# A bidirectional hybrid block on one core: transposes of FFN blocks grouped and moved behind the next gate job's first quantum, those of mLSTM outputs and merged branches grouped

## Chip, core and metric

One Trainium2 chip, one of its cores. The metric is the device time of one execution in microseconds (us). The engines are named as the profile names them: PE (TensorE, matmuls) with PEld (its weight loads), DVE (VectorE), ACT (ScalarE), POOL (GpSimd) and SP (SyncE, which issues most DMAs).

## What is computed

One layer over 256 tokens of width 2048, in float32. A mixer has two branches, a bidirectional mLSTM with 4 heads of width 512 and a bidirectional gated delta rule with 16 heads; their outputs are projected, gated, added and projected again. A SwiGLU feed-forward network (FFN) of inner width 5632 follows, then a final norm. Cut to what matters here:

```python
h_a = rms_norm(h_a, mlstm_norm_w)                       # 4 heads x 512
y_a = (sigmoid(a_o) * h_a) @ w_branch_a
x = x + gate_m * ((g_a * y_a + g_b * y_b) @ w_out)      # merged branches
hf = rms_norm(x, norm_ffn_w) * (1 + scale_f) + shift_f
gt, up = split(hf @ w_gate_up, 2)
x = x + gate_f * ((silu(gt) * up) @ w_down)
return rms_norm(x, norm_final_w)
```

## The kernel before

**Two forms of every number.** A product of two float32 matrices is made of three fast matmuls: each operand is split into a high part (rounded to the fast format) and a low part (the rest), and high x high, low x high and high x low are added. ACT makes the high part with a copy, DVE the low part with a subtraction. So weights arrive as `raw`, become `wh` and `wl` (L213, L215), and activations exist as pairs: `hah`/`hal` (mLSTM output), `mgh`/`mgl` (merged branches), `hfh`/`hfl` (FFN input), `ffh`/`ffl` (FFN inner activations). `split` (L290) makes such a pair from a tile in PSUM.

**Jobs and quanta.** `tjob` (L198) is one projection: all 256 tokens, as two halves of 128, by 512 output columns. For the gate and up projections it goes through 4 chunks of weights, each in two halves. One half is a *quantum*: one `wh`, one `wl` (three buffers each), and 12 matmuls with 512 columns (L247 high x high, L248 low activations x high weights, L249 high x low weights). After each quantum the generator calls `pump` and yields. `pump` (L159) hands out a side job: while the FFN runs, every 8 quanta one product on DVE of a row of `ada` with `crow` (L125), from which the gate row of the last residual is made.

**Transposes.** The result of a job has tokens on the partitions; the next projection needs features there. TensorE transposes each 128 x 128 block into a bank of PSUM (`gps`, L76, four banks, 512 float32 columns each), and ACT and DVE split it from there. Three places do so, each with 8 transposes for 512 features (4 feature blocks `f`, 2 token halves `t`):

- `mlstm` (L982), for each of 4 heads: tile `pxa`, transposes at L1061, then for each feature block a scaled copy on ACT to `hah` (L1065) and a multiply-subtract on DVE to `hal` (L1066). The four steps are written one block after another: two transposes, the copy, the subtraction, then the next block's two transposes, two blocks to a bank. The heads run in pairs (0 with 1, 2 with 3), interleaved piece by piece, beside the jobs `yb`.
- `merged` (L1174), for each of 4 column groups: tile `pxm`, transposes at L1181, called three times during the jobs `ya` (L1257) and once in the first job `o` (L1272). Four transposes to a bank, then a `split` of the bank (L291, L292).
- the FFN loop (L1522), for each of 11 blocks `j`: gate job, up job, then the product `sg` = silu(gate) x up on DVE (L1526, one for each token half), then tile `pxf`, transposes at L1532, four to a bank, and a `split` of each bank to `ffh` and `ffl`. Only the down projection (jobs `d`) reads these.

**What sets the order.** Each engine runs its own stream of instructions in order; engines wait for each other with semaphores. The order within a stream is made when the kernel is built, by a scheduler that plays the program through with its own model of times: of the instructions of an engine that it counts as ready, it takes the one written first. So an instruction that isn't ready there lets later ones pass. `order(ins)` (L72) pins an instruction behind the one written last before it on the same engine; `order(ins, False)` does nothing. Instructions on the same bank of PSUM are kept apart: one that writes into a bank is held until the reads written before it are done, even if they read other columns.

The lines as they stand in the FFN loop:

```python
run(gate(j) if j else gt0)
sg = sgs.pop(j)
run(tjob(f"up{j}", ..., lambda ps: [V.tensor_tensor(sg[:, t], sg[:, t], ps[t], ALU.mult) for t in range(2)]))
for e2 in range(2):
    px = gps(f"pxf{j}_{e2}")
    ...
```

Of the kernel before, what the change touches and what calls it, by code (L numbers as in the profile page):

```python
# [9 lines left out]
F32 = mybir.dt.float32  # L10
F32R = mybir.dt.float32r
AF = mybir.ActivationFunctionType
ALU = mybir.AluOpType
PSUM = bass.MemoryType.PSUM

P = 128
T = 256
# [15 lines left out]
PK_MNW = 128  # L33
# [19 lines left out]
def hybrid_block(ctx: ExitStack, tc: tile.TileContext, xr, nfr, crow, pk_d, cst_d, ada2, ada4, win0, winb, wint, wba, wbb, wo, wgu, wd, out, dbg=None):  # L53
    nc = tc.nc
    V, S, G, PE = nc.vector, nc.scalar, nc.gpsimd, nc.tensor

    def pool(stack, name, bufs=1, **kw):
        return stack.enter_context(tc.tile_pool(name=name, bufs=bufs, **kw))
# [10 lines left out]
    def big(p, dt, name):  # L69
        return p.tile([P, KB, T], dt, tag="b16", name=name)  # L70

    def order(ins, yes=True):  # L72

        return tc.keep_in_program_order(ins) if yes else ins

    def gps(name):  # L76
        return g_ps.tile([P, 512], F32, tag="g", name=name)
# [3 lines left out]
    pk = cp.tile([P, PK_N], F32, name="pk")  # L81
# [8 lines left out]
    ident = cst[:, CS_ID : CS_ID + P]  # L90
# [185 lines left out]
    def run(job):  # L276
        for _ in job:
            pass
# [11 lines left out]
    def split(hi, lo, v):  # L290
        S.activation(hi, v, AF.Copy)  # L291
        V.tensor_tensor(lo, v, hi.bitcast(F32), ALU.subtract)  # L292
# [214 lines left out]
    with ExitStack() as s0:  # L507
# [54 lines left out]
        for b2 in range(KB // 2):  # L562
            px = gps(f"pxx{b2}")
# [418 lines left out]
    def mlstm(h):  # L982
# [52 lines left out]
        hs = ml.tile([P, 2, DV_A], F32, tag="hs", bufs=2, name=f"hs{h}")  # L1035
# [17 lines left out]
        for t in range(2):  # L1053
            V.scalar_tensor_tensor(hs[:, t], hs[:, t], ss[:, t : t + 1], so[:, t], ALU.mult, ALU.mult)
        yield
        for e2 in range(2):
            px = gps(f"pxa{h}_{e2}")
            for e in range(2):
                f = 2 * e2 + e
                for t in range(2):  # L1060
                    PE.transpose(px[:, e * T + t * P : e * T + (t + 1) * P], hs[:, t, f * P : (f + 1) * P], ident)  # L1061
                b = 4 * h + f
                c = pk[:, PK_MNW + b : PK_MNW + b + 1]
                pe_ = px[:, e * T : (e + 1) * T]
                S.activation(hah[:, b], pe_, AF.Copy, scale=c)  # L1065
                V.scalar_tensor_tensor(hal[:, b], pe_, c, hah[:, b].bitcast(F32), ALU.mult, ALU.subtract)  # L1066
        yield

    heads1 = {h: gdn_phase1(h) for h in range(NH_B)}
# [25 lines left out]
    for g in range(4):  # L1095
# [6 lines left out]
        if g == 3:  # L1102
            settle()
            sf.close()
            mq["pool"] = pool(sq_, "mq", side="right")
            first2 = [mlstm(h) for h in range(2)]
            for c in first2:
                next(c)
            o4s = [o_load(0, mq["pool"])]
# [63 lines left out]

    def merged(g, mgh, mgl):  # L1174

        for e2 in range(2):
            px = gps(f"pxm{g}_{e2}")
            for e in range(2):
                f = 2 * e2 + e
                for t in range(2):  # L1180
                    PE.transpose(  # L1181
                        px[:, e * T + t * P : e * T + (t + 1) * P], mg[:, t, g * 512 + f * P : g * 512 + (f + 1) * P], ident
                    )
            b = 4 * g + 2 * e2
            split(mgh[:, b : b + 2], mgl[:, b : b + 2], px.rearrange("p (e t) -> p e t", e=2))

    def y_bs():
        for g in range(4):
# [23 lines left out]
    hah, hal = big(bigD, F32R, "hah"), big(bigD, F32R, "hal")  # L1212
    mg = mgp.tile([P, 2, D], F32, name="mg")
# [6 lines left out]
    drive(cores, 3)  # L1220
    every[0] = 1
    drive(steps(mlstm(2), mlstm(3)), 3)
    fill(1000)
    mgh, mgl = big(bigC, F32R, "mgh"), big(bigC, F32R, "mgl")
# [29 lines left out]
    for g in range(4):  # L1254
        for i, _ in enumerate(y_a(g)):
            if g and i == 3:
                merged(g - 1, mgh, mgl)  # L1257
            if i in (1, 5) and g < 2:
                row_diag(2, 2 * g + i // 4, sr)
            if i in (3, 7) and g < 2:  # L1260
                row_spread(2, 2 * g + i // 4, gm)
# [8 lines left out]
    for _ in range(2):  # L1270
        next(o_first)
    merged(3, mgh, mgl)  # L1272
    sw = ExitStack()
    sd.close()
# [45 lines left out]
    def gate_done(j):  # L1320
        def done(ps):
            sgs[j] = later["pool"].tile([P, 2, 512], F32, tag="sg", bufs=2, name=f"sg{j}")
            for t in range(2):
                S.activation(sgs[j][:, t], ps[t], AF.Silu)
        return done

    def gate(j):
        return tjob(f"gt{j}", [wgu[j, 0, u] for u in range(4)], Late("h"), Late("l"), gate_done(j), 0 if j else 2, steps=2, lead=None if j else xq)
# [9 lines left out]
    gt0 = gate(0)  # L1338
# [179 lines left out]
    ffh = fp.tile([P, FB, T], F32R, name="ffh")  # L1518
    ffl = fp.tile([P, FB, T], F32R, name="ffl")
    every[0] = 8  # L1520

    for j in range(FB // 4):  # L1522
        run(gate(j) if j else gt0)
        sg = sgs.pop(j)
        run(tjob(f"up{j}", [wgu[j, 1, u] for u in range(4)], hfh, hfl,
                 lambda ps: [V.tensor_tensor(sg[:, t], sg[:, t], ps[t], ALU.mult) for t in range(2)]))  # L1526
        for e2 in range(2):
            px = gps(f"pxf{j}_{e2}")
            for e in range(2):
                f = 2 * e2 + e  # L1530
                for t in range(2):
                    PE.transpose(px[:, e * T + t * P : e * T + (t + 1) * P], sg[:, t, f * P : (f + 1) * P], ident)  # L1532
            b = 4 * j + 2 * e2
            split(ffh[:, b : b + 2], ffl[:, b : b + 2], px.rearrange("p (e t) -> p e t", e=2))

    sh.close()
    dp = pool(ctx, "dp", side="right")
    gf = dp.tile([P, D], F32, name="gf")
# [30 lines left out]
    for g in range(4):  # L1569
        c = slice(g * 512, (g + 1) * 512)  # L1570
# [119 lines left out]
```

## Time and profile before

| | us |
|---|---|
| median of 3 runs | 1951.5 (1947.19 to 1954.09) |
| the profiled execution, its own time | 1949.33 |
| its span in the trace | 1947.5 |
| DVE busy | 1406.7 |
| ACT busy | 1033.8 |

The mean granted clock of TensorE in the profiled execution is 0.997 of full speed. The span reaches from the first to the last instruction of the trace. A line of the timeline reads: start in us, duration in us, engine, line of the kernel, operation, output tile <- input tiles, shapes, how many such in a row (xN), and in brackets how long the engine was idle before it and what it waited for. The durations of matmuls overlap, because they are pipelined; what one costs is read from start to start. A line of the waits reads: engine, tile and line, what it waited for, then the total in us, how many times, and the longest. The tile names are without the number of the block or head, so `pxf` is all of `pxf0_0` to `pxf10_1`.

### The profile page before, as it was taken

Reading aid. Unit: us, or ns where it says so; the run is one execution under the profiler, and the core shown is the slowest. Engines: PE = TensorE matmul, PEld = TensorE weight load, DVE = VectorE, ACT = ScalarE, POOL = GpSimd, SP = SyncE. Lnnn points to the kernel's source line nnn. Section 1 sums busy time; section 2 is a strip of 40 time slices with the busy share of each in tenths; the row PEclk is TensorE's granted clock in tenths of the full one; section 3 lists DMA queues with packets and bytes.
Section 4 is the critical chain, followed back from the end, with each engine's and each line's share of the span. In section 5 each row is a group of like instructions: output and inputs, shape, how many; then the busy total and the mean of one; then the engine's idle time right before and its main releaser. Section 6 shows DMA issues by size and latency. Waiting matters only on the chain.

```text
span 1947.5 us, 27217 instructions
## 1 busy us (share of the span) xinstructions
PE 1919.7 (99%) x10436; PEld 1699.3 (87%) x10436; DVE 1406.7 (72%) x2084; ACT 1033.8 (53%) x1564; POOL 124.1 (6%) x223
## 2 busy tenths in 40 slices
PE   8999999999999999999999999999999999999997
PEld 6888889998999899889788888888888888888886
DVE  6788886898788789876577988766666565555554
ACT  3147656775776587565544444644444444444443
POOL 0001220111011101120100000200000000000000
PEclk9999999999999999999999999999999999999999
DMA  9997676667676766686777998576667665655563
GB/s 399 420 358 236 188 256 249 214 224 238 219 220 204 241 220 238 208 293 245 268 289 266 351 353 314 195 263 245 246 239 260 239 219 199 204 207 209 196 208 137
DMA packets 80774, 485.68 MB, mean 249 GB/s; under 512 B 11434, under 2 KB 17138, under 8 KB 26626
## 3 DMA queue, kind: packets, MB, share of 16 engines
q1 hardware_dynamic: 64368, 451.02, 63.9%
q0 software_dynamic: 8672, 17.88, 4.3%
q10 hardware_dynamic: 7602, 15.03, 2.0%
q8 instruction: 82, 1.34, 0.3%
q14 instruction: 50, 0.40, 0.1%
HBM read 467.07 MB, written 16.82 MB: 248 GB/s over the span
## 4 chain that ended last, share of the span: by engine, by line
PE 90%; DMA 4%; DVE 3%; ACT 2%; issue 1%; SPq 0%; DVEq 0%; ACTq 0%
PE acc_up L247 4%; PE acc_up L249 4%; PE acc_up L248 4%; PE acc_gt L248 4%; PE acc_d L248 4%; PE acc_gt L249 4%; PE acc_d L247 4%; PE acc_d L249 4%; PE acc_gt L247 4%; DMA ra<-ada 3%; PE acc_b L186 3%; PE acc_o L247 3%; PE acc_o L248 3%; PE acc_o L249 3%; PE acc_b L188 3%; PE acc_b L187 3%
## 5 line engine op out<-in xcount | busy, mean ns | idle before, releaser
L215 DVE TENSOR_TENSOR wl_d<-raw_d,wh_d 128x1024 fp32r<-128x1024 f32 x88 | 107.7, 1225 | 105.9 <-ACT wh_d L213 105.9
L215 DVE TENSOR_TENSOR wl_up<-raw_up,wh_up 128x1024 fp32r<-128x1024 f32 x88 | 107.7, 1225 | 100.7 <-ACT wh_up L213 100.7
L215 DVE TENSOR_TENSOR wl_gt<-raw_gt,wh_gt 128x1024 fp32r<-128x1024 f32 x88 | 107.7, 1224 | 78.6 <-ACT wh_gt L213 78.6
L186 PE MATMUL acc_b<-hh,wh_b 128*128 128x256 f32 x576 | 161.9, 281 | 0.0
L213 ACT ACTIVATE wh_d<-raw_d 128x1024 fp32r<-128x1024 f32 x88 | 92.9, 1056 | 126.5 <-PE acc_d L248 117.7
L188 PE MATMUL acc_b<-hh,wl_b 128*128 128x256 f32 x576 | 158.7, 276 | 0.0
L187 PE MATMUL acc_b<-hl,wh_b 128*128 128x256 f32 x576 | 158.3, 275 | 0.0
L213 ACT ACTIVATE wh_gt<-raw_gt 128x1024 fp32r<-128x1024 f32 x88 | 92.8, 1055 | 117.1 <-PE acc_gt L248 71.1
L213 ACT ACTIVATE wh_up<-raw_up 128x1024 fp32r<-128x1024 f32 x88 | 92.7, 1055 | 108.1 <-PE acc_up L248 77.1
L125 DVE SCALAR_TENSOR_TENSOR ada<-ada,crow 128x2048 f32<-128x2048 f32 x64 | 146.2, 2284 | 0.0
L247 PE MATMUL acc_up<-wh_up,hfh 128*128 128x512 f32 x352 | 133.4, 379 | 0.0
L248 PE MATMUL acc_up<-wh_up,hfl 128*128 128x512 f32 x352 | 133.4, 379 | 0.0
L249 PE MATMUL acc_up<-wl_up,hfh 128*128 128x512 f32 x352 | 133.4, 379 | 0.0
L247 PE MATMUL acc_gt<-wh_gt,hfh 128*128 128x512 f32 x344 | 131.6, 383 | 0.0
L248 PE MATMUL acc_gt<-wh_gt,hfl 128*128 128x512 f32 x344 | 131.3, 382 | 0.2 <-DVE hfl L1475 0.2
L247 PE MATMUL acc_d<-wh_d,ffh 128*128 128x512 f32 x344 | 130.5, 379 | 0.0
L248 PE MATMUL acc_d<-wh_d,ffl 128*128 128x512 f32 x344 | 130.5, 379 | 0.0
L249 PE MATMUL acc_gt<-wl_gt,hfh 128*128 128x512 f32 x344 | 130.4, 379 | 0.0
L249 PE MATMUL acc_d<-wl_d,ffh 128*128 128x512 f32 x344 | 130.4, 379 | 0.0
L595 PE MATMUL first<-x,raw 128*128 128x256 f32 x488 | 110.1, 386 | 6.0 <-ACT x L587 6.0
L595 PEld LDWEIGHTS first<-x,raw 128*128 128x128 f32 x488 | 92.9, 192 | 23.3 <-ACT x L587 10.7
L187 PEld LDWEIGHTS acc_b<-hl,wh_b 128*128 128x128 f32 x576 | 110.6, 192 | 0.1
(403 smaller groups left out, 5294.7 us busy)
## 6 DMA issues: line engine op xcount, KB each, us to landing
ada<-ada SPq DMA_DIRECT2D x64, 1024.0 KB, 5.2
raw_gt<-wgu SPq DMA_DIRECT2D x44, 1024.0 KB, 5.0
raw_up<-wgu SPq DMA_DIRECT2D x44, 1024.0 KB, 5.0
raw_d<-wd SPq DMA_DIRECT2D x44, 1024.0 KB, 4.9
raw_b<-winb SPq DMA_DIRECT2D x36, 1024.0 KB, 5.6
ra<-ada SPq DMA_DIRECT2D x30, 1025.0 KB, 14.9
raw_z<-wint SPq DMA_DIRECT2D x16, 1024.0 KB, 5.0
raw_v<-wint SPq DMA_DIRECT2D x16, 1024.0 KB, 5.4
```

The lines of the kernel that those rows point to most:

```text
L125: order(V.scalar_tensor_tensor(raw, raw, 1.0, row_c[:, :D], ALU.mult, ALU.mult, accum_out=mod[:, c : c + 1]))
L186: PE.matmul(o, wh[:, k], woven(hh[:, kk]), start=kk == 0, stop=False)
L187: PE.matmul(o, wh[:, k], woven(hl[:, kk]), start=False, stop=False)
L188: PE.matmul(o, wl[:, k], woven(hh[:, kk]), start=False, stop=kk == KB - 1)
L213: order(S.activation(wh, raws[u][:, k0 : k0 + 2], AF.Copy), early)
L215: order(V.tensor_tensor(wl, raws[u][:, k0 : k0 + 2], wh.bitcast(F32), ALU.subtract), early or beside[0])
L247: order(PE.matmul(ps[t], xh[:, kk, c], woven(wh[:, k]), start=kk == 0, stop=False), early and steps > 1)
L248: PE.matmul(ps[t], xl[:, kk, c], woven(wh[:, k]), start=False, stop=False)
L249: PE.matmul(ps[t], xh[:, kk, c], woven(wl[:, k]), start=False, stop=kk == last)
L595: PE.matmul(first[o], raw[:, o], x[:, b], start=b == 0 and o % 2 == 0, stop=b == KB - 1 and o % 2 == 1)
```

## The change

In `mlstm` and `merged` the two banks are taken first, all 8 transposes are written in one go, and the reads follow. Within a group every transpose but the first is pinned with `order` behind the one before it (`f or t` is false only for the first). In the FFN loop the transposes and their `split` become a function `turn`, put aside in `turning`; it is called in the next round of the loop after the gate job's first quantum, that is at its first yield. The turn of the last block is called right after the loop.

```diff
@@ mlstm
-        for e2 in range(2):
-            px = gps(f"pxa{h}_{e2}")
-            for e in range(2):
-                f = 2 * e2 + e
-                for t in range(2):
-                    PE.transpose(px[:, e * T + t * P : e * T + (t + 1) * P], hs[:, t, f * P : (f + 1) * P], ident)
-                b = 4 * h + f
-                c = pk[:, PK_MNW + b : PK_MNW + b + 1]
-                pe_ = px[:, e * T : (e + 1) * T]
-                S.activation(hah[:, b], pe_, AF.Copy, scale=c)
-                V.scalar_tensor_tensor(hal[:, b], pe_, c, hah[:, b].bitcast(F32), ALU.mult, ALU.subtract)
+        px = [gps(f"pxa{h}_{i}") for i in range(2)]
+        for f in range(4):
+            for t in range(2):
+                c = (f % 2) * T + t * P
+                order(PE.transpose(px[f // 2][:, c : c + P], hs[:, t, f * P : (f + 1) * P], ident), f or t)
+        for f in range(4):
+            b = 4 * h + f
+            c = pk[:, PK_MNW + b : PK_MNW + b + 1]
+            pe_ = px[f // 2][:, (f % 2) * T : (f % 2 + 1) * T]
+            S.activation(hah[:, b], pe_, AF.Copy, scale=c)
+            V.scalar_tensor_tensor(hal[:, b], pe_, c, hah[:, b].bitcast(F32), ALU.mult, ALU.subtract)
@@ merged
-        for e2 in range(2):
-            px = gps(f"pxm{g}_{e2}")
...
-            b = 4 * g + 2 * e2
-            split(mgh[:, b : b + 2], mgl[:, b : b + 2], px.rearrange("p (e t) -> p e t", e=2))
+        px = [gps(f"pxm{g}_{i}") for i in range(2)]
+        for f in range(4):
+            for t in range(2):
+                c = (f % 2) * T + t * P
+                order(PE.transpose(px[f // 2][:, c : c + P], mg[:, t, g * 512 + f * P : g * 512 + (f + 1) * P], ident), f or t)
+        for i in range(2):
+            b = 4 * g + 2 * i
+            split(mgh[:, b : b + 2], mgl[:, b : b + 2], px[i].rearrange("p (e t) -> p e t", e=2))
@@ FFN loop
+    turning = []
 
     for j in range(FB // 4):
-        run(gate(j) if j else gt0)
+        for i, _ in enumerate(gate(j) if j else gt0):
+            if turning and not i:
+                turning.pop()()
         sg = sgs.pop(j)
         run(tjob(f"up{j}", [wgu[j, 1, u] for u in range(4)], hfh, hfl,
                  lambda ps: [V.tensor_tensor(sg[:, t], sg[:, t], ps[t], ALU.mult) for t in range(2)]))
-        for e2 in range(2):
-            px = gps(f"pxf{j}_{e2}")
...
-            split(ffh[:, b : b + 2], ffl[:, b : b + 2], px.rearrange("p (e t) -> p e t", e=2))
+
+        def turn(j=j, sg=sg):
+            px = [gps(f"pxf{j}_{i}") for i in range(2)]
+            for f in range(4):
+                for t in range(2):
+                    c = (f % 2) * T + t * P
+                    order(PE.transpose(px[f // 2][:, c : c + P], sg[:, t, f * P : (f + 1) * P], ident), f or t)
+            for i in range(2):
+                b = 4 * j + 2 * i
+                split(ffh[:, b : b + 2], ffl[:, b : b + 2], px[i].rearrange("p (e t) -> p e t", e=2))
+
+        turning.append(turn)
+
+    turning.pop()()
```

More of the change, by code (lines that the diff above doesn't have):

```diff
@@ L1174, in merged @@
     def merged(g, mgh, mgl):
-        for e2 in range(2):
-            px = gps(f"pxm{g}_{e2}")
[L1178 to L1183, printed above, removed]
-            b = 4 * g + 2 * e2
-            split(mgh[:, b : b + 2], mgl[:, b : b + 2], px.rearrange("p (e t) -> p e t", e=2))
+        px = [gps(f"pxm{g}_{i}") for i in range(2)]
[6 more added lines that the diff above has]
+            split(mgh[:, b : b + 2], mgl[:, b : b + 2], px[i].rearrange("p (e t) -> p e t", e=2))
     def y_bs():
@@ L1526, in hybrid_block @@
                  lambda ps: [V.tensor_tensor(sg[:, t], sg[:, t], ps[t], ALU.mult) for t in range(2)]))
-        for e2 in range(2):
-            px = gps(f"pxf{j}_{e2}")
-            for e in range(2):
-                f = 2 * e2 + e
+        def turn(j=j, sg=sg):
+            px = [gps(f"pxf{j}_{i}") for i in range(2)]
+            for f in range(4):
                 for t in range(2):
-                    PE.transpose(px[:, e * T + t * P : e * T + (t + 1) * P], sg[:, t, f * P : (f + 1) * P], ident)
-            b = 4 * j + 2 * e2
-            split(ffh[:, b : b + 2], ffl[:, b : b + 2], px.rearrange("p (e t) -> p e t", e=2))
+                    c = (f % 2) * T + t * P
[5 more added lines that the diff above has]
+    turning.pop()()
     sh.close()
```

## The prediction

> **What bounds the kernel now.** I read the page first, then who TensorE (PE) and its weight loader (PEld) waited for, then the timeline around the transposes.
>
> ```profile
> span 1947.5 us, 27217 instructions
> PE 1919.7 (99%) x10436; PEld 1699.3 (87%) x10436; DVE 1406.7 (72%) x2084; ACT 1033.8 (53%) x1564; POOL 124.1 (6%) x223
> PE 90%; DMA 4%; DVE 3%; ACT 2%; issue 1%; SPq 0%; DVEq 0%; ACTq 0%
> ```
>
> TensorE is busy for 1919.7 of 1947.5 us and carries 90% of the chain that ended last. So a change counts only if it alters what passes through TensorE, or makes it wait. The two waits that touch the edited transposes are these (waits of PEld: total us, times, longest):
>
> ```profile
> PEld pxf L1532 <- DVE sg L1526: 4.2, 11, 0.4
> PEld pxa L1061 <- DVE hal L1066: 0.8, 2, 0.4
> ```
>
> Together 5.0 us, 0.26% of the span, and part of it is work that would pass anyway. No row names the transposes of merged branches (pxm). The timeline of one FFN block shows what a wait costs:
>
> ```profile
> 1280.39 1.28 DVE L1526 TENSOR_TENSOR sg<-sg,acc_up 128x512 f32<-128x512 f32 x2
> ...
> 1280.77 0.38 PE L247 MATMUL acc_gt<-wh_gt,hfh 128*128 128x512 f32 x1
> ...
> 1281.13 0.44 PE L1532 MATMUL pxf<-cst,sg 128*128 128x128 f32 x2
> ...
> 1281.33 0.46 PE L248 MATMUL acc_gt<-wh_gt,hfl 128*128 128x512 f32 x1
> ...
> 1281.63 0.38 PE L249 MATMUL acc_gt<-wl_gt,hfh 128*128 128x512 f32 x1
> ...
> 1281.84 1.23 DVE L215 TENSOR_TENSOR wl_gt<-raw_gt,wh_gt 128x1024 fp32r<-128x1024 f32 x1 [0.17 <-ACT wh_gt L213]
> 1281.84 0.82 PE L1532 MATMUL pxf<-cst,sg 128*128 128x128 f32 x6
> 1282.37 1.09 ACT L291 ACTIVATE ffh<-pxf 128x512 fp32r<-128x512 f32 x2 [0.56 <-PE pxf L1532]
> ...
> 1282.42 0.46 PE L247 MATMUL acc_gt<-wh_gt,hfh 128*128 128x512 f32 x1
> ...
> 1282.72 0.38 PE L248 MATMUL acc_gt<-wh_gt,hfl 128*128 128x512 f32 x1
> ...
> 1283.00 1.29 DVE L292 TENSOR_TENSOR ffl<-pxf,ffh 128x512 fp32r<-128x512 f32 x2
> ...
> 1284.21 2.28 DVE L125 SCALAR_TENSOR_TENSOR ada<-ada,crow 128x2048 f32<-128x2048 f32 x1
> ...
> 1284.43 1.06 ACT L213 ACTIVATE wh_gt<-raw_gt 128x1024 fp32r<-128x1024 f32 x1 [0.97 <-PE acc_gt L248]
> ...
> 1286.41 0.08 DVE L125 DVE_READ_ACCUMULATOR ada<-ada,crow 128x1 f32 x1
> 1286.41 1.22 DVE L215 TENSOR_TENSOR wl_gt<-raw_gt,wh_gt 128x1024 fp32r<-128x1024 f32 x1
> ...
> 1287.90 0.38 PE L248 MATMUL acc_gt<-wh_gt,hfl 128*128 128x512 f32 x1
> ```
>
> From 1282.72 to 1287.90 lie 24 undisturbed matmuls: 5.18 / 24 = 0.216 us each, the **pitch**. From 1280.77 to 1282.72 are 1.95 us for four matmuls (0.86) and eight transposes, so the eight cost **1.09**. They wait for the product sg (1280.39 + 1.28 for both halves): after the matmul of 1280.77 the next start would be 1280.99, but the transposes start at 1281.13, 0.14 lost. They come as two and six, and behind each group the second matmul follows 0.30 after the first (1281.33 to 1281.63, 1282.42 to 1282.72), 0.08 over the pitch. So leaving transposes costs 0.08 each time.
>
> **mLSTM heads.** The timeline of TensorE, heads 0 and 1, then 2 and 3:
>
> ```profile
> 977.26 0.38 PE L249 MATMUL acc_yb<-wl_yb,obh 128*128 128x512 f32 x1
> 977.48 1.04 PE L1061 MATMUL pxa<-cst,hs 128*128 128x128 f32 x8
> 978.27 0.46 PE L247 MATMUL acc_yb<-wh_yb,obh 128*128 128x512 f32 x1
> 978.57 0.38 PE L248 MATMUL acc_yb<-wh_yb,obl 128*128 128x512 f32 x1
> ...
> 979.87 0.38 PE L248 MATMUL acc_yb<-wh_yb,obl 128*128 128x512 f32 x1
> 980.23 0.44 PE L1061 MATMUL pxa<-cst,hs 128*128 128x128 f32 x2
> ...
> 982.03 0.38 PE L247 MATMUL acc_yb<-wh_yb,obh 128*128 128x512 f32 x1
> ```
>
> ```profile
> 1051.74 0.38 PE L249 MATMUL acc_yb<-wl_yb,obh 128*128 128x512 f32 x1
> 1051.95 1.04 PE L1061 MATMUL pxa<-cst,hs 128*128 128x128 f32 x8
> ...
> 1053.05 0.38 PE L248 MATMUL acc_yb<-wh_yb,obl 128*128 128x512 f32 x1
> ...
> 1053.91 0.38 PE L249 MATMUL acc_yb<-wl_yb,obh 128*128 128x512 f32 x1
> 1054.33 0.44 PE L1061 MATMUL pxa<-cst,hs 128*128 128x128 f32 x2
> ...
> 1056.04 0.38 PE L247 MATMUL acc_yb<-wh_yb,obh 128*128 128x512 f32 x1
> ```
>
> Here a **run of eight** can be priced: 977.26 to 978.57 is 1.31, less two pitches, **0.88** (1051.74 to 1053.05 gives the same); inside, 0.79 / 8 = 0.099 per transpose. The other eight are broken up by matmuls, since the code writes each block's reads (hah, hal) ahead of the next block's transposes into the same bank, and these wait for hal. 979.87 to 982.03 is 2.16 for five matmuls: 1.08. In the second pair 1053.91 to 1056.04 is 2.13 for four: 1.27.
>
> **The change, part by part.** Nothing is added or removed: the same transposes, copies and DMAs run. Their order changes.
>
> *FFN, ten of eleven blocks.* The turn is written behind the next gate job's first quantum, 12 matmuls, 12 x 0.216 = 2.59 us. The product ends 1281.67, the quantum 1280.77 + 2.59 = 1283.36: no wait is left, and with all eight ready, pinned behind one another and written ahead of the second quantum, they form one run. 1.09 becomes 0.88: 0.21 x 10 = **2.1 us**.
>
> What gets late: ACT's two copies (1.09) and DVE's two subtractions (1.29), which only the down projection reads. On ACT the copy wh for the fourth quantum waits for the first quantum's buffer, today until 1284.43, then until about 1283.4: with its 1.06 and the 1.09 it is done by 1285.6. Behind the subtractions on DVE stands wl for the same quantum. DVE is free at 1281.84 + 1.23 = 1283.07, when no transposed block is there yet; so the product with ada, 2.28 + 0.08 for reading its sum, can go ahead, where it stood behind ffl; then 1.29 and 1.22: 1287.9. TensorE wants this wl at 1283.36 + 0.88 + 24 x 0.216 = 1289.4. So 1.5 us of cover; I cost it at nothing. The turn issues no DMA and passes no SP or POOL instruction. Both sg buffers are used as before: the next gate writes its own only seven quanta later.
>
> *Last block.* It is turned right behind its job, so the wait stays. The second transpose (t = 1) now waits for the second product instead of a t = 0 one going first: one transpose, 0.1, leaves the time that is lost anyway. Between -0.1 and +0.2 (one more exit of 0.08 and the 0.1); I take **+0.1**.
>
> *mLSTM.* All eight of a head go ahead of its reads, into the four banks already used at once. Two heads in one run of sixteen cost 16 x 0.099 + 0.08 = 1.67; as two runs 1.76. Now: 0.88 + 1.08 = 1.96 and 0.88 + 1.27 = 2.15. Won: 0.29 + 0.48 = **0.8 us**, at least 0.6.
>
> *Merged branches.* All four already run as eight, so I take nothing:
>
> ```profile
> 1093.81 1.04 PE L1181 MATMUL pxm<-cst,mg 128*128 128x128 f32 x8
> ...
> 1116.27 1.04 PE L1181 MATMUL pxm<-cst,mg 128*128 128x128 f32 x8
> ...
> 1137.86 1.04 PE L1181 MATMUL pxm<-cst,mg 128*128 128x128 f32 x8
> ...
> 1154.28 1.04 PE L1181 MATMUL pxm<-cst,mg 128*128 128x128 f32 x8
> ```
>
> **Sum:** 2.1 + 0.8 - 0.1 = 2.8 us off. The profiled execution took 1949.3 us (span 1947.5 and 1.8 around it): 1946.5. The median of the runs shown, 1951.5, lies 2.2 above it: **1948.7**. Ends: if only the wait of 0.14 goes and no run closes, 10 x 0.14 = 1.4. The most is all 120 transposes of FFN and mLSTM at 0.099 with nothing around them: 11 x 1.09 + 1.96 + 2.15 = 16.1 against 11.9, so 4.2 off.
>
> The Trainium skill, "TensorE: Matmul & The Clock Gate", section "LDWEIGHTS (loading the stationary operand)", gives a weight load as columns / 1.2 ns, so 107 ns for 128, and every transpose here loads its own weights; by an estimate from it a run of eight is 8 x 0.107 + 0.08 = 0.94, and the sum 2.1 off. The trace has 0.099, so it decides.
>
> **Rivals.**
>
> *Runs do not close (0.09).* The pins keep an order, not neighbours: if the scheduler counts a later transpose as not ready, matmuls slip in as now. Then 1.4: 1950.1. For it: two and six today. Against: the quantum's 1.7 us of margin.
>
> *The change does not do what it says (0.04).* If the scheduler places the turn where it stands today, nothing moves: 1951.5.
>
> *DVE turns late (0.07), the slower side.* Place: wl of the gate's fourth quantum, behind ada and ffl. It decides when DVE's work there passes 4.9 + 1.5 = 6.4 us. A second ada product in the same gap (2.36) would make wl 0.9 late in each of ten blocks: +9, less 2.8, gives 1957.7. Against: one product in this gap.
>
> *The clock falls (0.01).* If transposes counted as idleness and the 12 matmuls behind each of ten runs went at half speed, 10 x 2.59 = +26: 1975. The Trainium skill says this of transposes, same page, section "Part 4: PE-mode transpose": they do not count as PE-busy the same way. Against: behind today's run of eight at 977.48 the matmuls keep their pitch by 978.57, at most 0.08 over.
>
> *More than the path holds (0.09).* Beyond 4.2 only a rearrangement elsewhere or scatter remains, since the scheduler's later choices may shift with the earlier ones: 1944.
>
> **How the numbers follow.** The forecast has 0.70. A change under 0.3%, 5.9 us, is about what a measurement of this kernel cannot tell from none; the runs shown spread over 1947.2 to 1954.1. Faster by more (below 1945.6): half of the last rival, 0.05, and 0.07 of scatter around the forecast: 0.12. Slower by more: DVE and clock 0.08, and 0.02 of scatter: 0.10. Within: 0.78. The range takes the ends 1.4 and 4.2, 1950.1 to 1947.3, and some 3.5 us of scatter each way: 1943.8 to 1953.8.
>
> **What would show it.** Right: PEld's wait of pxf for sg falls from 11 times to one; eight pxf in one row of the timeline, about 2.6 us behind the gate's first matmul; a block's period 0.2 shorter; pxa waits for no hal. Wrong: TensorE waiting for wl_gt from DVE in the fourth quantum, transposes still in twos, or a period that does not shrink though the runs close.

## The result, and the profile after

The changed kernel takes 1947.7 us (median of 14 runs, 1945.99 to 1949.88), the kernel before 1950.7 beside it (14 runs, 1947.19 to 1954.73): a ratio of 0.9984 (0.9977 to 0.9992), 3.0 us off, 1.6 to 4.5 by the interval. The forecast was 2.8 off and 1948.7 us; no difference above 0.3%, as forecast.

The two profiled executions hide this: 1949.30 us now (span 1947.4) and 1949.33 before (1947.5). So the stages must be compared. The waits of PEld that name the edited transposes have shrunk to the one line of the last FFN block; none names pxa and hal any more:

```profile
PEld pxf L1534 <- DVE sg L1527: 0.4, 1, 0.4
```

The page of the changed kernel has TensorE as full as before:

```profile
span 1947.4 us, 27209 instructions
PE 1920.7 (99%) x10436; PEld 1704.7 (88%) x10436; DVE 1406.5 (72%) x2084; ACT 1032.7 (53%) x1564; POOL 124.1 (6%) x223
```

The timeline of the first FFN block after the change, the counterpart of the one in the prediction:

```profile
1283.89 1.23 DVE L215 TENSOR_TENSOR wl_gt<-raw_gt,wh_gt 128x1024 fp32r<-128x1024 f32 x1 [0.17 <-ACT wh_gt L213]
...
1285.04 2.28 DVE L125 SCALAR_TENSOR_TENSOR ada<-ada,crow 128x2048 f32<-128x2048 f32 x1
1285.19 0.38 PE L249 MATMUL acc_gt<-wl_gt,hfh 128*128 128x512 f32 x1
...
1285.39 1.06 ACT L213 ACTIVATE wh_gt<-raw_gt 128x1024 fp32r<-128x1024 f32 x1 [1.53 <-PE acc_gt L248]
1285.41 1.04 PE L1534 MATMUL pxf<-cst,sg 128*128 128x128 f32 x8
...
1286.20 0.46 PE L247 MATMUL acc_gt<-wh_gt,hfh 128*128 128x512 f32 x1
...
1286.36 1.07 ACT L291 ACTIVATE ffh<-pxf 128x512 fp32r<-128x512 f32 x2
1286.50 0.38 PE L248 MATMUL acc_gt<-wh_gt,hfl 128*128 128x512 f32 x1
...
1287.24 1.28 DVE L292 TENSOR_TENSOR ffl<-pxf,ffh 128x512 fp32r<-128x512 f32 x2
...
1288.45 1.22 DVE L215 TENSOR_TENSOR wl_gt<-raw_gt,wh_gt 128x1024 fp32r<-128x1024 f32 x1
...
1291.90 0.38 PE L249 MATMUL acc_gt<-wl_gt,hfh 128*128 128x512 f32 x1
```

All eight transposes stand in one row, where two and six stood. From 1285.19 to 1286.50 are 1.31, less two pitches of 0.216: they cost 0.88. On DVE the product with ada now stands ahead of the subtractions (ffl), as foretold, and the fourth quantum's wl is written by 1288.45 + 1.22 = 1289.67, 2.2 us before the matmul at 1291.90 that reads it first.

The stretch from the first of the ten moved groups to the last, nine periods, by the windows view: the changed kernel, then the kernel before (stretch; its length; then busy times, granted clock, DMA):

```profile
1285.41:1666.25 380.84, 380.84 (x1801) 334.04 (x1800) 229.78 (x213) 169.75 (x181) 0.00 (x0) 1.00 0.68 238
```

```profile
1281.13:1663.82 382.69, 382.69 (x1801) 332.70 (x1801) 230.41 (x214) 170.69 (x181) 0.00 (x0) 1.00 0.67 236
```

42.316 us a block against 42.521: 0.205 less, or **2.05 us** in ten blocks. The same number of matmuls passes at the same clock in 1.85 us less.

The mLSTM heads, from the timeline of TensorE in the changed kernel:

```profile
979.80 0.38 PE L249 MATMUL acc_yb<-wl_yb,obh 128*128 128x512 f32 x1
980.02 1.91 PE L1060 MATMUL pxa<-cst,hs 128*128 128x128 f32 x16
981.68 0.46 PE L247 MATMUL acc_yb<-wh_yb,obh 128*128 128x512 f32 x1
981.98 0.38 PE L248 MATMUL acc_yb<-wh_yb,obl 128*128 128x512 f32 x1
...
1054.28 1.91 PE L1060 MATMUL pxa<-cst,hs 128*128 128x128 f32 x16
...
1063.79 0.38 PE L247 MATMUL acc_ya<-wh_ya,hah 128*128 128x512 f32 x1
```

Sixteen in a row: 979.80 to 981.98 is 2.18, less two pitches 1.75. Two such pairs cost 3.50, where 1.96 + 2.15 = 4.11 stood: 0.61 less. The whole stage gives the same. From the matmul ahead of the first transpose to the first matmul of ya it took 977.26 to 1061.87 before, 84.61, and takes 979.80 to 1063.79, 83.99: **0.6 us**.

So 2.05 + 0.6 = 2.7 us are gone. The spans are equal all the same, because the matmul ahead of the first pxa started 2.54 us later in this execution (979.80 for 977.26), and because 0.13 more passed from the first matmul of ya to the first gate matmul of the block shown (219.03 for 218.90). At 1705.98 both traces are level again. Up to the first pxa TensorE's instructions stand in the same order in both kernels, so the change didn't make the 2.54: two of the kernels below that are the kernel before up to there (the FFN part alone, and the one that reads x1) reach that matmul at 979.11 and 979.00. Runs of the kernel before alone lie 7.5 us apart.

### The profile page after: what moved, and what is told of

Its sections match the earlier page's. It is cut to its first block, busy times and chain, and to the rows that moved or that the text cites. A ratio compares the mean times of both kernels' runs of the same rounds, so it can differ in the third digit from the quotient of the medians.

```text
span 1947.4 us, 27209 instructions
## 1 busy us (share of the span) xinstructions
PE 1920.7 (99%) x10436; PEld 1704.7 (88%) x10436; DVE 1406.5 (72%) x2084; ACT 1032.7 (53%) x1564; POOL 124.1 (6%) x223
## 4 chain that ended last, share of the span: by engine, by line
PE 88%; DVE 4%; DMA 4%; ACT 2%; issue 1%; POOL 0%; SPq 0%; DVEq 0%; POOLq 0%
PE acc_up L249 4%; PE acc_up L248 4%; PE acc_up L247 4%; PE acc_gt L248 4%; PE acc_d L248 4%; PE acc_gt L249 4%; PE acc_d L247 4%; PE acc_d L249 4%; PE acc_gt L247 4%; DMA ra<-ada 3%; PE acc_b L186 3%; PE acc_b L188 3%; PE acc_b L187 3%; PE acc_o L247 2%; PE acc_o L249 2%; PE acc_o L248 2%
```

## The experiments

My theory after the result was that of the prediction: an FFN turn had lost 0.14 to the wait for sg and 0.08 to a second exit from transposes into matmuls, and a long run is cheap (0.099 per transpose). The first rival: there is no price for leaving transposes, and all 0.21 is the wait. The second: the cover on DVE is thin, so the gain hangs on it. Each run's median is given with that of the kernel before on the same chip.

**One part at a time.** *Moved only*: the turn behind the first quantum, with the old inner loop and no pins, all else as before.

```diff
         def turn(j=j, sg=sg):
-            px = [gps(f"pxf{j}_{i}") for i in range(2)]
...
+            for e2 in range(2):
+                px = gps(f"pxf{j}_{e2}")
...
```

> The FFN turn stands behind the gate's first quantum, but its eight transposes are written as before (bank by bank, nothing pinned); mLSTM and merged branches as before. Theory (moving suffices: behind the quantum all eight are ready, so the scheduler lets them pass together): ten turns as a run of eight, period of a block 42.32 us as in the changed kernel, 2.0 to 2.1 us off before. Rival (the pins close the run): transposes still in groups, period 42.38 or more, 1.4 us off at most. mLSTM unchanged: 8 together, then groups of two.

1948.0 against 1950.9, 0.9985 (0.9976 to 0.9994). All ten groups run as eight in a row without pins, the first at 1283.36 and the last at 1664.20: a period of 42.316, that of the changed kernel. The moving alone gives the FFN's whole gain.

*Grouped only*: the FFN's eight transposes written in one go and pinned, at the old place.

```diff
+        px = [gps(f"pxf{j}_{i}") for i in range(2)]
+        for f in range(4):
+            for t in range(2):
+                c = (f % 2) * T + t * P
+                order(PE.transpose(px[f // 2][:, c : c + P], sg[:, t, f * P : (f + 1) * P], ident), f or t)
```

> The FFN transposes are written together and pinned, but at their old place ahead of the gate job; mLSTM and merged branches as before. Theory (the place decides): every block becomes one transpose, matmuls, seven transposes, like the last block of the changed kernel (1.07 us for the eight), so the period stays 42.50 to 42.52 and the time within 0.2 us of before. Rival (closing the run is what gains): all eight behind the wait, 0.88 + 0.14 = 1.02, period 42.45, 0.7 us off.

1950.6 against 1950.9, 1.0003 (0.9994 to 1.0012). The groups are now one and seven, the wait stays, and the first groups of the ten stand at 1279.27 to 1661.96: (1661.96 - 1279.27) / 9 = 42.52, the old period.

```profile
PEld pxf L1531 <- DVE sg L1526: 4.2, 11, 0.4
```

*The mLSTM part alone, and the FFN part alone:*

```diff
-        for e2 in range(2):
-            px = gps(f"pxa{h}_{e2}")
...
+        px = [gps(f"pxa{h}_{i}") for i in range(2)]
...
```

> Only the mLSTM transposes are grouped; FFN and merged branches as before. Theory: two runs of sixteen at 1.75 us instead of 1.96 and 2.15, so TensorE reaches the first matmul with hah 0.6 us earlier, counted from the matmul before the first run; 0.1 of it is lost again at a wait for wl_ya from DVE before the first merged transposes; time 0.5 us off before, which the total cannot tell from nothing. Rival (the mLSTM heads carry more than a third of the gain, through what follows them): 1 us or more off.

1951.2 against 1950.9, 1.0002 (0.9993 to 1.0011). The stage took 84.00 here, 0.6 less, but the total can't show 0.03%.

```diff
-        for e2 in range(2):
-            px = gps(f"pxf{j}_{e2}")
...
+        turning.append(turn)
```

> The whole FFN part of the change (moved, together, pinned); mLSTM and merged branches as before. Theory: period 42.32, ten blocks 2.0 to 2.1 us off before, last block 1.07 as before or 1.09; the sum of this and the mLSTM part alone is the whole change. Rival (the parts help each other): less than 1.5 us off.

1947.3 against 1950.9, 0.9986 (0.9976 to 0.9997). What the total shows of the change is the FFN part.

**The wait alone.** The kernel before, whose FFN transposes read x1, which is long ready, in place of sg:

```diff
-                    PE.transpose(px[:, e * T + t * P : e * T + (t + 1) * P], sg[:, t, f * P : (f + 1) * P], ident)
+                    PE.transpose(px[:, e * T + t * P : e * T + (t + 1) * P], x1[:, t, f * P : (f + 1) * P], ident)
```

> The kernel before, with one edit: the FFN transposes read x1, the residual, which has long been ready, instead of sg; so the inner activations of the FFN are not the reference's, and the number and the place of the transposes stay. Theory (only the wait for sg ever cost anything, a transpose costs 0.11 wherever it stands): 0.2 off in each of eleven blocks, 2.3 us off before, period 42.32, as with the move. Rival (the place behind the quantum gains something of its own): less than 1 us off.

1947.5 against 1950.7, 0.9989 (0.9979 to 0.9999). Nothing is moved, and the eight close up at the old place by themselves:

```profile
1282.41 0.38 PE L249 MATMUL acc_up<-wl_up,hfh 128*128 128x512 f32 x1
1282.63 1.04 PE L1532 MATMUL pxf<-cst,x 128*128 128x128 f32 x8
1283.42 0.46 PE L247 MATMUL acc_gt<-wh_gt,hfh 128*128 128x512 f32 x1
1283.72 0.38 PE L248 MATMUL acc_gt<-wh_gt,hfl 128*128 128x512 f32 x1
```

0.88 again. The last of the ten is at 1663.47: a period of 42.316. The wait is the whole 0.21; two and six was what it looked like. How the 0.21 is spread over the two late groups, the recorded starts don't tell.

**Does leaving transposes cost?** In the changed kernel, the eight are spread one by one behind each third matmul of the second and third quanta, pinned there:

```diff
+                    if weave:
+                        weave.pop(0)()
...
+            weave.extend(lambda f=f, t=t: one(f, t) for f in range(4) for t in range(2))
```

> The changed kernel with the FFN turn pulled apart: behind the first quantum one transpose follows each group of three matmuls, so eight single transposes spread over the second and third quantum, all pinned; the copies and subtractions follow the eighth. Theory (leaving transposes costs 0.08 each time, the transpose itself 0.10): 8 x 0.18 = 1.44 for a block's eight instead of 0.88, 0.56 x 10 = 5.6 us slower than the changed kernel, 2.6 slower than before. Rival (only the wait for sg mattered, transposes cost the same wherever they stand): the same time as the changed kernel, period 42.32.

1946.9 against 1950.1, 0.9982 (0.9973 to 0.9990): eight exits a block in place of one, and next to nothing lost. The period, from the first single of the first block (1286.63) to that of the tenth (1667.63), is 42.33, 0.02 over that of the changed kernel; seven more exits at 0.08 would have put it 0.56 over. The timeline of TensorE in this kernel:

```profile
1286.41 0.38 PE L249 MATMUL acc_gt<-wl_gt,hfh 128*128 128x512 f32 x1
1286.63 0.27 PE L1539 MATMUL pxf<-cst,sg 128*128 128x128 f32 x1
1286.65 0.46 PE L247 MATMUL acc_gt<-wh_gt,hfh 128*128 128x512 f32 x1
1286.95 0.38 PE L248 MATMUL acc_gt<-wh_gt,hfl 128*128 128x512 f32 x1
1287.17 0.38 PE L249 MATMUL acc_gt<-wl_gt,hfh 128*128 128x512 f32 x1
1287.38 0.27 PE L1539 MATMUL pxf<-cst,sg 128*128 128x128 f32 x1
1287.41 0.46 PE L247 MATMUL acc_gt<-wh_gt,hfh 128*128 128x512 f32 x1
```

The matmul behind a single transpose is recorded 0.02 after it, and the next one 0.30 after that. From one transpose to the next are 0.76 (1286.63 to 1287.38), less three pitches 0.11. So a transpose costs 0.11 alone, 0.88 / 8 = 0.11 in eights and 1.75 / 16 = 0.11 in sixteens. The 0.08 of exit is a piece of the transpose that the recorded starts put behind the next matmul. My theory falls; the first rival stands.

**How much cover has DVE?** Four, then eight more operations on DVE in each turn, ahead of its `split`, on sg as output:

```diff
+            for i in range(4):
+                V.tensor_tensor(sg[:, i % 2], sg[:, i % 2], sg[:, 1 - i % 2], ALU.max)
             for i in range(2):
```

> The changed kernel with four more DVE operations of 128x512 in every turn, some 0.6 us each and 2.45 in all, on the sg tile after its transposes have read it; nothing reads the result. They stand ahead of the subtractions ffl and so ahead of wl of the gate's fourth quantum. By the prediction's cover of 1.5 us (from the end of that wl to the first matmul of its quantum) wl is 0.95 late in each of ten blocks: 9 us slower than the changed kernel. Theory now: in the changed kernel's trace wl ends at 1289.67, and the first matmul that reads it is the third of its quantum, at about 1291.9, so the cover is 2.2 and the loss 0.25 a block, 2 to 3 us; TensorE is seen waiting for wl_gt. Rival (DVE is covered much further, by the three buffers): no loss at all.

> As with four, but eight more DVE operations in every turn, 4.9 us. Theory: 4.9 less the cover of 2.2 is 2.7 a block, 27 us slower than the changed kernel, all of it as TensorE waiting for wl_gt in the fourth quantum. By the prediction's cover of 1.5: 34 us slower. Rival (covered): under 5 us slower.

1948.5 and 1947.9 against 1950.1, 0.9985 (0.9975 to 0.9994) and 0.9987 (0.9978 to 0.9996). Neither tests what it was made for. DVE's timeline of the second one:

```profile
1285.45 0.68 DVE L292 TENSOR_TENSOR ffl<-pxf,ffh 128x512 fp32r<-128x512 f32 x1
1286.05 0.68 DVE L1536 TENSOR_TENSOR sg<-sg 128x512 f32<-128x512 f32 x1
1286.65 1.22 DVE L215 TENSOR_TENSOR wl_gt<-raw_gt,wh_gt 128x1024 fp32r<-128x1024 f32 x1
1287.79 0.68 DVE L1536 TENSOR_TENSOR sg<-sg 128x512 f32<-128x512 f32 x1
1288.39 1.22 DVE L215 TENSOR_TENSOR wl_gt<-raw_gt,wh_gt 128x1024 fp32r<-128x1024 f32 x1
```

Each operation needs the one before it, so when one isn't ready the scheduler lets a wl pass: they fill DVE's holes. So the wl was pinned behind the added work, which is written behind the gate's third quantum:

```diff
+            if j and i == 2:
+                for m in range(4):
+                    order(V.tensor_tensor(sg[:, m % 2], sg[:, m % 2], sg[:, 1 - m % 2], ALU.max))
+            beside[0] = bool(j and i == 2)
```

> The four extra DVE operations per block once more (0.6 us each, on sg after its transposes, read by nobody), now written behind the gate's third quantum, with wl of the fourth pinned behind them, in the ten blocks that are turned late. In the changed kernel's trace the subtractions before that wl end at about 1288.45, the four add 2.4 and wl 1.2: 1292.1, against about 1291.9 when TensorE wants it. Theory (cover of 2.2 us): late by 0.2 to 0.3 a block, 2 to 3 us slower than the changed kernel, TensorE waiting for wl_gt. By the prediction's cover of 1.5: 9 us slower. Rival (DVE is covered further than that): no loss.

1952.7 against 1950.7, 1.0010 (1.0001 to 1.0019): 5 us above the changed kernel by the ratios, where 2 to 3 were expected. Its waits of TensorE, and then its timeline, with DVE's added work, the late wl and the matmul that reads it:

```profile
PE acc_gt L249 <- DVE wl_gt L215: 3.4, 8, 0.4
```

```profile
1288.56 2.86 DVE L1527 TENSOR_TENSOR sg<-sg 128x512 f32<-128x512 f32 x4
1291.34 3.49 DVE L215 TENSOR_TENSOR wl_gt<-raw_gt,wh_gt 128x1024 fp32r<-128x1024 f32 x3
...
1291.80 0.38 PE L248 MATMUL acc_gt<-wh_gt,hfl 128*128 128x512 f32 x1
1292.61 0.48 PE L249 MATMUL acc_gt<-wl_gt,hfh 128*128 128x512 f32 x1 [0.43 <-DVE wl_gt L215]
```

The wl starts 2.78 later than it would (1288.56 to 1291.34); its reader, due at 1291.80 + 0.22 = 1292.02, comes at 1292.61, 0.59 late. 2.78 - 0.59 = 2.2 of cover, the figure read above from the changed kernel. The loss is twice what was expected because the four operations take 2.78 and not 2.4.

With eight operations in place of four:

```diff
-                for m in range(4):
+                for m in range(8):
```

> As with four pinned, but eight: 4.8 us ahead of wl of the fourth quantum. Theory: 2.6 late a block, 26 us slower than the changed kernel, about 1974, as ten waits of TensorE for wl_gt of 2.6 each. By the prediction's cover: 33 us slower. Rival (covered further): under 5 us slower.

1986.1 against 1950.7, 1.0187 (1.0166 to 1.0207), 40 us above the changed kernel by the ratios, where 26 were expected, and more than the wait explains:

```profile
PE acc_gt L249 <- DVE wl_gt L215: 27.2, 10, 3.0
```

The rest is the clock, in the last section.

**The last block too.** In the changed kernel, the last turn is called behind the first quantum of the down projection's first job:

```diff
+    d_first = tjob("d0", [wd[0, u] for u in range(KD)], ffh, ffl, lambda *q: done_d(*q))
+    next(d_first)
     turning.pop()()
```

> The changed kernel with the last block's turn moved as well, behind the first quantum of the down projection's first job; the pool of the FFN tiles closes and the gate row is made after that. Theory: the last of the eleven waits for sg goes, 0.2 us; 1947.5, which the total cannot tell from the changed kernel, but PEld shows no wait of pxf for sg. Rival (what follows, the gate row's products and matmuls, comes late and is waited for): 1 us or more slower than the changed kernel.

1946.5 against 1950.7, 0.9984 (0.9975 to 0.9994). The last wait is gone and the last eight run in a row at 1707.16. That is worth what one block is, 0.2 us, and can't be told from the changed kernel in the total.

## Why the prediction was right, and where its working was wrong

- **FFN, 2.1 off: right in size and place** (2.05). The quantum covers the product, the eight run in a row 2.59 us behind the gate's first matmul (1282.82 to 1285.41), and a block's period is 0.205 shorter.
- **Its working failed at "So leaving transposes costs 0.08 each time" and at "0.099 per transpose".** The 0.88 of a run and the 1.09 of a block were true differences between matmuls outside the group; the splits of them were read off starts inside it. No exit is saved (singles: 0.11 each, no loss), and the wait was 0.21, not 0.14 (the kernel that reads x1: period 42.316). So "if only the wait of 0.14 goes and no run closes" was no lower case: when the wait goes, all goes, run or no run. The forecast stood since 0.21 had been measured whole.
- **The weight of the Trainium skill's figure was judged wrongly.** "The trace has 0.099, so it decides" set a step between starts inside the group against a price. The runs have 0.11 for one, eight and sixteen. The Trainium skill, "TensorE: Matmul & The Clock Gate", section "LDWEIGHTS (loading the stationary operand)", gives 107 ns for the weight load of 128 columns, and 0.11 agrees with it. That the load is what sets the price, no run here shows. The sum by that figure was also added up wrongly: 2.1 leaves out the last block's 0.1, with which it is 2.0.
- **mLSTM, 0.8: the mechanism right, the size 0.6.** A run of sixteen was taken at 1.67 and measured 1.75: again 0.099 for 0.11. The "at least 0.6" holds. What went is the wait for hal; by 0.11 each, the two broken-up eights had cost 1.08 and 1.27 where 0.88 is work, 0.20 + 0.39 over. So here grouping helps, but because it writes the transposes ahead of the reads of their bank. That the wait is its whole gain is argued from the rows; only the part as a whole was run.
- **Last block, +0.1: it cost nothing.** It runs as one and seven as foretold, and from 1705.98 to 1708.13 are 2.15 for five matmuls and eight transposes: 2.15 - 5 x 0.216 = 1.07, against 1.09 in a block before.
- **Merged branches, nothing: right.** They run as four eights, as before.
- **DVE's cover: 2.2, not 1.5.** The wl was 0.3 earlier than worked out, and its first reader is the third matmul of its quantum, not the first: 0.43. The order of ada and ffl on DVE was right.
- **The rivals.** Runs do close, and the change does what it says. *DVE turns late* is a real mechanism and didn't occur: it decides at 4.9 + 2.2 = 7.1 us of DVE work, not at 6.4, and past that the block gets longer: with four operations wl was 0.59 late, the period 43.02 in place of 42.32, and eight of the ten blocks waited, 5 us in all. *The clock falls* didn't occur for transposes: behind eight and sixteen in a row the matmuls keep 0.216.
- **The total is nearer than its terms.** 0.8 for mLSTM was 0.2 too much and the last block's 0.1 was not lost; the two misses cancel in part, and that is luck. The forecast time, 1948.7, lies 1.0 above the 1947.7 measured, 0.8 of it because it started from three runs with a median of 1951.5, where fourteen give 1950.7.

## What to carry to other kernels

A consumer that stalls a full engine is cured by putting independent work of that engine ahead of it; grouping alone does nothing while the producer is late, and no pins were needed once it wasn't. Price a small operation between undisturbed matmuls outside its group (elapsed time, less the matmuls' pitch, by the count), never from starts inside it; then what is left over a known price was, here, the wait. To test whether a wait is the cause, feed the instruction something that is ready; to test cover, pin the added work ahead of the consumer, or the scheduler may file it into the holes, as it did here.

## What the runs showed of the hardware that I had not expected

The clock of TensorE fell to about half behind some gaps of 2.9 us. TensorE in the kernel with eight pinned operations:

```profile
1289.41 0.38 PE L248 MATMUL acc_gt<-wh_gt,hfl 128*128 128x512 f32 x1
1292.70 0.92 PE L249 MATMUL acc_gt<-wl_gt,hfh 128*128 128x512 f32 x2 [2.91 <-DVE wl_gt L215]
1293.42 0.63 PE L247 MATMUL acc_gt<-wh_gt,hfh 128*128 128x512 f32 x1
1293.84 0.63 PE L248 MATMUL acc_gt<-wh_gt,hfl 128*128 128x512 f32 x1
...
1296.40 0.41 PE L248 MATMUL acc_gt<-wh_gt,hfl 128*128 128x512 f32 x1
1296.65 0.38 PE L249 MATMUL acc_gt<-wl_gt,hfh 128*128 128x512 f32 x1
```

```profile
1289.00:1292.60 3.60, 0.79 (x4) 0.36 (x2) 3.50 (x6) 0.80 (x1) 0.00 (x0) 1.00 0.01 2
1292.70:1296.00 3.30, 3.30 (x9) 2.65 (x10) 2.22 (x2) 0.16 (x1) 0.00 (x0) 0.55 0.63 216
```

Behind the gap the pitch is 0.42 and the granted clock 0.55, until 1296.40: ten matmuls in 3.95 us, 1.79 over their 2.16. But two blocks of the same kernel have the same gap and no dip, this one among them:

```profile
1387.06 0.70 PE L249 MATMUL acc_gt<-wl_gt,hfh 128*128 128x512 f32 x2 [2.91 <-DVE wl_gt L215]
```

```profile
1387.10:1390.40 3.30, 3.30 (x15) 2.90 (x16) 2.56 (x3) 1.06 (x1) 0.00 (x0) 1.00 0.71 218
```

Eight of the ten blocks have a gap of 2.9 to 3.0 us; six show the half clock behind it and two do not, nor do the last two blocks, with gaps of 1.9. A period with the dip is 47.18 and one without is 45.49. Six times 1.69 are some 10 us: over the ten blocks the wait is 27.2 of some 40 us, and this is most of the rest. So a wait of 3 us on TensorE can cost more than 3 us. The Trainium skill, "TensorE: Matmul & The Clock Gate", section "HAM oscillation — how this bites in real kernels", puts the idle gap that does this above about 3.4 us; here 2.9 by the record, 3.29 from start to start (1289.41 to 1292.70), sufficed in six blocks of eight. What decides in which, no run here shows.

The clock can also dip with no gap in TensorE's records. The windows view of the kernel before, then of the kernel with the FFN grouped only, over the same stretch of the mLSTM stage (granted clock third from the end):

```profile
1005.00:1020.00 15.00, 15.00 (x71) 12.48 (x70) 7.78 (x13) 5.14 (x7) 0.00 (x0) 0.89 0.59 211
```

```profile
1005.00:1020.00 15.00, 15.00 (x75) 11.99 (x74) 9.46 (x14) 5.23 (x7) 0.00 (x0) 1.00 0.72 263
```

TensorE is busy throughout in both, and the first has four matmuls fewer: 0.11 x 15 = 1.65 us by the clock. The mLSTM stage took 82.91 in the second kernel and 84.61 in the first, although its code there is the same. Such a dip is 2.7 times the 0.6 that the change gives in this stage; the 0.6 was read from two executions that both have it (granted clock 0.98 over the stage). All thirteen traces bear the 0.6 out, like compared with like: with the dip the stage takes 84.60 or 84.61 with the old mLSTM code and 83.99 or 84.00 with the new; without it 82.91 and 83.08 with the old, 82.30 and 82.31 with the new. The slow matmuls begin 1.0 to 1.6 us behind 24 matmuls with one column each (L1029 in the kernel before), which fill 2.59 us (1006.21 to 1008.80 in the kernel before): 24 columns in all, where one ordinary matmul has 512. The 24 stand there in all thirteen traces, and nine have the dip. Whether they bring it about, and why it comes in one execution and not in the other, the runs do not show.
